# The split activations of a two-layer encoder trunk moved to multiples of 512 bytes in SBUF

## Chip, cores and metric

The kernel runs on one core of one Trainium2 chip. The metric is the device time of one execution in microseconds, over three runs; lower is better.

## The reference, cut to what matters

Two layers work on 256 tokens of 1024 channels in float32. Each layer is a half-weighted SwiGLU feed-forward, a mixer, and a second half-weighted feed-forward; a norm ends the trunk.

```python
def swiglu(x, w_gate, w_up, w_down):
    return (jax.nn.silu(x @ w_gate) * (x @ w_up)) @ w_down      # 1024 -> 2816 -> 1024
...
for l in range(DEPTH):                                           # DEPTH = 2
    x = x + RES_HALF * swiglu(rmsnorm(x, norm_ffn1[l]), ffn1_w_gate[l], ffn1_w_up[l], ffn1_w_down[l])
    h = rmsnorm(x, norm_mix[l])
    gq, gk, gv, gz, gb, ga, c_q, c_kv, k_rope, gate_logits = split_cols(h @ w_in[l])     # 1024 -> 4784
    y_a = gdn_branch(...)     # gated delta rule, both directions, then @ gdn_proj (512 -> 1024)
    y_b = mla_branch(...)     # latent attention (@ mla_w_uq, @ mla_w_ukv), then @ mla_proj (512 -> 1024)
    gates = sigmoid(gate_logits)
    x = x + (gates[:, :, 0] * y_a + gates[:, :, 1] * y_b) @ w_out[l]
    x = x + RES_HALF * swiglu(rmsnorm(x, norm_ffn2[l]), ffn2_w_gate[l], ffn2_w_up[l], ffn2_w_down[l])
return rmsnorm(x, final_norm)
```

## The kernel before, in words

Every large product is made of three float32r passes. An activation a is kept as a high and a low part (`split`, lines 101 to 109), a weight w too (`weights`, lines 111 to 127), and `mm3` (lines 129 to 135) adds a_hi w_hi, a_hi w_lo and a_lo w_hi in PSUM for one chunk of 128 channels and one tile of 128 tokens. In each pass the activation's 128x128 block is the stationary operand, which a weight load (PEld in the profile) brings into TensorE, and the weights' 128 rows of up to 512 columns are the moving operand, which the matmul (PE) streams. TensorE loads the block of the next pass while the columns of this one stream.

The activations lie channel-major: `xh`, `xl` (the normed trunk, 8 chunks of 256 tokens), `hh`, `hl` (the feed-forward's hidden layer, 22 chunks), and the eight `fr2` buffers of the mixer (two chunks each, `fr` in the profile), which hold the latents, the attention's output, the delta rule's output and the merged branches in turn. `to_chan` and `to_chan2` make them with TensorE transposes followed by `split`.

A feed-forward goes through the 2816 hidden columns in blocks of 512: gate, up, transposes into `hh` and `hl`. Then two products with w_down follow, 512 columns each, of 22 chunks x 2 token tiles x 3 passes. The last feed-forward's down products are in `finale`, whose second one takes the weights of its last six chunks from buffers in a pool `fin` of its own (`down(1, second, tail=6, pool=fin)`, line 303). The mixer's products with `xh` are `dense` and `qkv_group`; those with `fr2` are `mla_dense` (latents), and near the mixer's end the calls of `dense_t` on `oT` and `gT` and of `dense_halves` on `yT`. The order of the program's calls in the mixer is written out by hand (lines 980 to 1053); a planner in the framework then places the instructions of each engine by simulated due times.

Weights come through SyncE's DMA queue into `raw` (three buffers), ScalarE writes the high part (line 122), VectorE the low part (line 123).

Pools take SBUF one behind the other: `const`, `main`, `wpool`, `small`; then `ffn` or `mix`, which are opened and closed in turn and begin at the same byte; and `fin` behind `ffn`. Within a pool, tiles lie in the order in which they are first asked for, each rounded up to 32 bytes. The program places these tiles at the following bytes of each partition:

| tile | pool | begins at | past a multiple of 512 |
| --- | --- | --- | --- |
| `ident` | const | 17248 | 352 |
| `x_sb` | main | 23040 | 0 |
| `xh`, `xl` | main | 31232, 39424 | 0 |
| `whi` (3), `wlo` (3) | wpool | from 72192, steps of 4096 | 0 |
| first tile of `small`, which takes 576 bytes | small | 96768 | 0 |
| `hh`, `hl` | ffn | 97344, 119872 | 64 |
| `h` (4) | ffn | from 150592, steps of 2048 | 64 |
| `fr2` (8) | mix | from 181856, steps of 2048 | 96 |
| `whi` (3), `wlo` (3) of the finale | fin | from 171072 and 183360, steps of 4096 | 64 |

One chunk of 128 tokens is 512 bytes, one 128x512 block of weights 2048 bytes, so that each operand of a 512-column pass keeps the remainder of its tile.

Of the kernel before, what the change touches and what calls it, by code (L numbers as in the profile page):

```python
# [11 lines left out]
F32 = mybir.dt.float32  # L12
# [8 lines left out]
P = 128  # L21
D = 1024
S = 256
# [14 lines left out]
def encoder_trunk(ctx: ExitStack, tc: tile.TileContext, x, positions, norm_ffn1, ffn1_w_gate, ffn1_w_up,  # L38
# [23 lines left out]
    # the tensor engine's clock rises while the first loads run  # L62
# [8 lines left out]
    # columns of gains: ffn1 (8 per layer), mix, ffn2, q latent (3), kv latent (2), gdn (1)  # L71
# [21 lines left out]
    xh = main.tile([P, NKC, S], F32R, name="xh")  # L93
    xl = main.tile([P, NKC, S], F32R, name="xl")
# [6 lines left out]
    def split(hi, lo, ps, gain=None):  # L101
        """hi + lo = gain * ps, both exact in float32r."""
        if gain is None:
            A.copy(out=hi, in_=ps)
            V.tensor_tensor(out=lo, in0=ps, in1=hi.bitcast(F32), op=ALU.subtract)
        else:
            A.activation(out=hi, in_=ps, func=AF.Copy, scale=gain)  # L107
            V.scalar_tensor_tensor(out=lo, in0=ps, scalar=gain, in1=hi.bitcast(F32), op0=ALU.mult,  # L108
                                   op1=ALU.subtract)

    def weights(src, nk, w, pool=wpool):
        """A [nk*128, w] slice of weights, as (hi, lo) tiles of up to 1024 elements a partition."""
        raw = wpool.tile([P, 2048], F32, tag="raw", name="raw", bufs=3)
        nc.sync.dma_start(out=raw[:, :nk * w].rearrange("p (k c) -> p k c", c=w),
                          in_=src.rearrange("(k p) c -> p k c", p=P))
        per = 1024 // w
        res = []
        for k0 in range(0, nk, per):
            n = min(per, nk - k0)
            hi = pool.tile([P, 1024], F32R, tag="whi", name="whi", bufs=3)  # L120
            lo = pool.tile([P, 1024], F32R, tag="wlo", name="wlo", bufs=3)
            A.copy(out=hi[:, :n * w], in_=raw[:, k0 * w:(k0 + n) * w])  # L122
            V.tensor_tensor(out=lo[:, :n * w], in0=raw[:, k0 * w:(k0 + n) * w], in1=hi[:, :n * w].bitcast(F32),  # L123
                            op=ALU.subtract)
            for k in range(n):
                res.append((hi[:, k * w:(k + 1) * w], lo[:, k * w:(k + 1) * w]))
        return res

    def mm3(ps, a, w, n, start, stop, ts=range(NT)):
        """ps[t] (+)= a^T w in three passes, for the token tiles ts."""  # L130
        for t in ts:
            a1, a2 = (v[:, t * P:(t + 1) * P] for v in a)
            T.matmul(ps[t][:, :n], lhsT=a1, rhs=w[0], start=start, stop=False)  # L133
            T.matmul(ps[t][:, :n], lhsT=a1, rhs=w[1], start=False, stop=False)  # L134
            T.matmul(ps[t][:, :n], lhsT=a2, rhs=w[0], start=False, stop=stop)  # L135

    def dense_t(acts, src, c0, w, evac, tail=4, pool=wpool):
        """evac(t, psum [128 tokens, w]) of acts @ src[:, c0:c0+w]; acts: (hi, lo) [128, tokens] of each chunk.
        The last chunks (tail or fewer) go through for one token tile, then for the other."""
# [19 lines left out]
    def dense(ah, al, nk, src, c0, w, evac, **kw):  # L159
        dense_t([(ah[:, k, :], al[:, k, :]) for k in range(nk)], src, c0, w, evac, **kw)  # L160

    def dense_halves(acts, parts):
        """dense_t for two parts (src, c0, evac) of 512 columns: the first half of the chunks for both, then the second."""
# [11 lines left out]
    def to_chan(srcs, hi, lo, kc, gain0=None):  # L175
        """Transposes srcs[t] ([128 tokens, n*128]) into chunks kc.. of hi / lo [128, chunk, tokens]."""
        n = srcs[0].shape[1] // P
        for j in range(0, n, 2):
# [6 lines left out]
            if gain0 is None:  # L185
                split(hi[:, kc + j:kc + j + m, :], lo[:, kc + j:kc + j + m, :],
                      pt[:, :m * S].rearrange("p (c s) -> p c s", s=S))
            else:
                for i in range(m):
                    g = gain0 + j + i  # L190
                    split(hi[:, kc + j + i, :], lo[:, kc + j + i, :], pt[:, i * S:(i + 1) * S], gcol[:, g:g + 1])
# [7 lines left out]
    def x_done(t, cg):  # L199
        """Half cg of x's tile t is final: sum of squares."""  # L200
        A.activation(out=junk, in_=x_sb[:, t, cg * 512:(cg + 1) * 512], func=AF.Square,
                     accum_out=state["ss"][:, t, cg:cg + 1])
# [28 lines left out]
    def ffn(w_gate, w_up, w_down, next_gain, hook=None):  # L231
# [3 lines left out]
        with tc.tile_pool(name="ffn", bufs=1) as fp:  # L235
            hh = fp.tile([P, NFC, S], F32R, name="hh")
            hl = fp.tile([P, NFC, S], F32R, name="hl")
            for c0 in range(0, DFF, 512):
# [17 lines left out]
                else:  # L256
                    dense_halves([(xh[:, k, :], xl[:, k, :]) for k in range(NKC)],
# [12 lines left out]
    def finale(down):  # L270
        """The last x, its norm, the result; x of the first half lies by its gains before the second is there."""
# [37 lines left out]
    def mixer_consts(tmp):  # L309
# [16 lines left out]
        alog = const.tile([P, depth, 8], F32, name="alog")  # -exp(A_log)  # L326
# [12 lines left out]
        # m[p, f]  # L339
# [6 lines left out]
        # half[:, 0]: partition % 32 < 16, half[:, 1]: the others  # L346
# [7 lines left out]
        # the off-diagonal 16-blocks of the 32-blocks on the diagonal: below it (mlo) and above it (mup)  # L354
# [11 lines left out]
        # rotary tables  # L366
# [42 lines left out]
    def mixer(l, next_gain):  # L409
# [7 lines left out]
        with tc.tile_pool(name="mix", bufs=1) as mp:  # L417
# [5 lines left out]

            def fr2():
                return mp.tile([P, 2, S], F32R, tag="fr2", name="fr2", bufs=8)
# [8 lines left out]
            def rstd_row():  # L434
                """rstd along the free axis, the same in every partition."""
# [26 lines left out]
            def to_chan2(srcs, gains):  # L462
                """Chunks of 128 channels, two to a tile: a list of (hi, lo) [128, tokens]."""
                n = srcs[0].shape[1] // P
                res = []
                for j in range(0, n, 2):
# [13 lines left out]
                    res += [(hi[:, i, :], lo[:, i, :]) for i in range(m)]  # L480
# [18 lines left out]
            def gdn_scalars():  # L499
# [4 lines left out]
                # softplus(a) = max(a, 0) + log1p(exp(-|a|))  # L504
# [14 lines left out]
            qkT = mp.tile([P, 8, S], F32, name="qkT")  # L519
            vT = {}  # lies in ysb until ysb is written  # L520
# [4 lines left out]
            def qkv_group(grp):  # L525
                """Two of the twelve chunks of channels."""
# [3 lines left out]
                # one group of sums after the other: they share a bank. The second takes the weights from the last on  # L530
                for c in range(2):
                    cc = slice(c * P, (c + 1) * P)
                    terms = [m for kc, (wh, wlo) in enumerate(ws)
                             for m in ((wh, xh[:, kc, :]), (wh, xl[:, kc, :]), (wlo, xh[:, kc, :]))]
                    for i, (w, a) in enumerate(terms[::-1] if c else terms):
                        T.matmul(pc[:, c], lhsT=w[:, cc], rhs=a, start=(i == 0), stop=(i == len(terms) - 1))  # L536
# [16 lines left out]
                # 2 silu(.); the lengths and |k| v below take account of the 2  # L553
# [5 lines left out]
            def lengths(c0):  # L559
                """1/|.| of four of the eight heads of q and k, a column for each head."""  # L560
                pss = gdp()[:, :4 * NT * 32].rearrange("p (c t s) -> p c t s", c=4, t=NT)
                for c in (0, 2):
# [3 lines left out]
                    for g in range(4):  # L566
                        # the sums for the tokens of group g, in each of its partitions
# [28 lines left out]
            def mla_dense(hf):  # L596
                """q, k, v of four heads, token-major, rotary parts turned."""
# [22 lines left out]
            def mla_heads(q, k, v):  # L620
                """attend(pair of heads), of the four that q, k, v hold."""
# [15 lines left out]
                def attend(c):  # L637
# [36 lines left out]
                    oT.append((hi[:, c, :], lo[:, c, :]))  # L674
# [4 lines left out]
            LA, Z, egc, cs = {}, {}, {}, {}  # L679
            LAd = {}  # L680
            for d in range(2):
                LAd[d] = mp.tile([P, NT, NH, 2, P], F32, name=f"LA{d}")  # [.., 0, :] for q, [.., 1, :] for k
# [7 lines left out]
            def gdn_coeffs():  # L690
# [3 lines left out]
                # -beta / |k|^2  # L694
# [17 lines left out]
            def gdn_decay(t):  # L712
                """E[j, h, i]: decay from token j to token i of the tile, 0 where i comes before j."""
                for d in range(2):
# [10 lines left out]
                    if t == d:  # L725
                        # first tile of this direction: decay of each token up to the carried state
# [5 lines left out]
                    # hi_m[p, f] holds where f is at or after p in this direction  # L732
# [25 lines left out]
            def gdn_base():  # L758
                """XC, ZC: inverses (and transposes) of the 16-blocks on the diagonal, each block in a partition of its
                own meanwhile."""  # L760
# [47 lines left out]
            def inv_zero():  # L808
                """Z = X^T = (1 + L)^-T from the inverted 16-blocks: blocks of 32, 64, 128 in turn."""
# [23 lines left out]
            def inv2(d):  # L833
# [9 lines left out]
                # the 64-block that the last step takes X from  # L843
# [41 lines left out]
            def gdn_first(d):  # L885
                """First tile of direction d: its solution, and what it adds to the other tile."""
# [39 lines left out]
            def gdn_out(t):  # L926
# [10 lines left out]
                # o here is -|q| sqrt(128) times the true one, zs_t is 2 silu(z) / rstd  # L937
# [118 lines left out]
    new_norm()  # L1056
    state["squares"] = False  # of the input: once its products run
# [32 lines left out]
```

## Time and profile before

| | us |
| --- | --- |
| median of the three runs | 1267.02 |
| lowest and highest | 1266.68, 1269.48 |
| span of the profiled execution, first to last instruction | 1260.2 |
| the median less that span | 6.8 |
| TensorE busy in the span | 1230.4 |
| VectorE busy | 774.1 |
| ScalarE busy | 623.4 |
| GpSimd busy | 132.5 |

The runs shown give a time for the median only; the profiled execution is known by its span, and what lies around a span (start and end of the program) is taken as the 6.8 us above. A matmul's recorded duration (390 ns for 512 columns) overlaps the next one's, so the pace of the matmuls is read from their start times. Nothing else runs on the core.

### The profile page before, as it was taken

How to read it: one execution, taken by the hardware profiler on the slowest of the kernel's cores; microseconds unless marked ns; L12 is line 12 of the kernel's file. 1: busy time of each engine (PE TensorE's matmuls, PEld its weight loads, DVE VectorE, ACT ScalarE, POOL GpSimd, SP SyncE). 2: the span in 40 equal slices, each digit the busy share in tenths (PEclk: the TensorE clock that was granted, in tenths of full speed). 3: DMA queues.
4: the chain of work that ended last, by engine and by line, in shares of the span. 5: the costliest groups of instructions: out<-in, count | busy, mean ns of one | idle time of the engine just before them, and what ended most of it. 6: DMA issues, size and time to landing. Idle time of an engine off the chain costs nothing.

```text
span 1260.2 us, 17612 instructions
## 1 busy us (share of the span) xinstructions
PE 1230.4 (98%) x7064; PEld 1031.9 (82%) x7064; DVE 774.1 (61%) x1127; ACT 623.4 (49%) x911; POOL 132.5 (11%) x237
## 2 busy tenths in 40 slices
PE   9999999899999999999999999998999999999997
PEld 6888889777988788888888888897778787888886
DVE  5655556986757665554555554588876576555554
ACT  6554445546445455443445443465555455544443
POOL 1000001445001000000000000015540000000010
PEclk9999999999999999999999999999999999999999
DMA  7554554435222555555555555543442245565552
GB/s 266 175 197 153 198 184 157 153 119 167 71 99 95 164 176 181 187 169 198 182 187 182 185 167 201 177 147 123 150 162 74 68 134 184 168 199 179 188 184 84
DMA packets 114576, 202.70 MB, mean 161 GB/s; under 512 B 4107, under 2 KB 30399, under 8 KB 114495
## 3 DMA queue, kind: packets, MB, share of 16 engines
q1 hardware_dynamic: 114031, 200.52, 47.8%
q8 instruction: 55, 0.90, 0.3%
q10 hardware_dynamic: 464, 1.06, 0.2%
q14 instruction: 26, 0.21, 0.1%
HBM read 200.52 MB, written 1.05 MB: 160 GB/s over the span
## 4 chain that ended last, share of the span: by engine, by line
PE 88%; DVE 4%; POOL 4%; issue 1%; ACT 1%; DMA 0%; POOLq 0%; SPq 0%; ACTq 0%
PE acc L133 24%; PE acc L134 23%; PE acc L135 23%; PE acc L536 4%; PE ms L183 2%; DVE wlo L123 2%; POOL bt L783 1%; PE ms L671 1%; PE ms L642 1%; POOL t L785 1%; PE gd L134 1%; PE gd L135 1%; PE gd L133 1%; PE gd L912 1%; DVE cv L551 1%
## 5 line engine op out<-in xcount | busy, mean ns | idle before, releaser
L123 DVE TENSOR_TENSOR wlo<-raw,whi 128x1024 fp32r<-128x1024 f32 (+3 forms) x388 | 471.2, 1217 | 371.0 <-ACT whi L122 369.0
L122 ACT CAST whi<-raw 128x1024 fp32r<-128x1024 f32 (+3 forms) x388 | 398.8, 1031 | 435.9 <-PE acc L135 392.0
L134 PE MATMUL acc<-wlo,xh 128*128 128x512 f32 (+3 forms) x968 | 360.7, 374 | 0.0
L135 PE MATMUL acc<-whi,xl 128*128 128x512 f32 (+3 forms) x968 | 357.5, 372 | 0.0
L133 PE MATMUL acc<-whi,xh 128*128 128x512 f32 (+3 forms) x968 | 344.9, 376 | 0.1
L134 PEld LDWEIGHTS acc<-wlo,xh 128*128 128x128 f32 x968 | 182.4, 188 | 29.8 <-issue 0.4
L133 PEld LDWEIGHTS acc<-whi,xh 128*128 128x128 f32 x968 | 181.4, 188 | 30.4 <-ACT xh L107 0.8
L135 PEld LDWEIGHTS acc<-whi,xl 128*128 128x128 f32 x968 | 182.1, 188 | 29.3
L134 PE MATMUL acc<-wlo,hh 128*128 128x512 f32 x352 | 138.9, 395 | 0.0
L135 PE MATMUL acc<-whi,hl 128*128 128x512 f32 x352 | 138.7, 394 | 0.0
L133 PE MATMUL acc<-whi,hh 128*128 128x512 f32 x352 | 129.1, 397 | 0.0
L135 PEld LDWEIGHTS acc<-whi,hl 128*128 128x128 f32 x352 | 65.9, 187 | 16.1
L133 PEld LDWEIGHTS acc<-whi,hh 128*128 128x128 f32 x352 | 65.9, 187 | 15.9
L134 PEld LDWEIGHTS acc<-wlo,hh 128*128 128x128 f32 x352 | 65.9, 187 | 15.3
L133 PE MATMUL acc<-whi,fr 128*128 128x512 f32 (+1 forms) x152 | 60.9, 407 | 9.2 <-DVE pre L543 7.9
L134 PE MATMUL acc<-wlo,fr 128*128 128x512 f32 (+1 forms) x152 | 61.0, 404 | 0.0
L135 PE MATMUL acc<-whi,fr 128*128 128x512 f32 (+1 forms) x152 | 58.2, 400 | 2.3 <-DVE fr L108 2.3
L536 PE MATMUL acc<-xl,whi 128*128 128x256 f32 x192 | 55.6, 289 | 0.0
L536 PE MATMUL acc<-xh,whi 128*128 128x256 f32 x192 | 55.5, 291 | 0.0
L536 PE MATMUL acc<-xh,wlo 128*128 128x256 f32 x192 | 53.3, 288 | 0.0
L551 DVE SCALAR_TENSOR_TENSOR cv<-pre,ccol,cv 128x256 f32<-128x256 f32 x96 | 51.6, 569 | 0.0
L246 ACT ACTIVATE sil<-acc,rstd 128x512 f32<-128x512 f32 (+1 forms) x48 | 31.0, 654 | 29.5 <-PE acc L135 29.4
(298 smaller groups left out, 1273.3 us busy)
## 6 DMA issues: line engine op xcount, KB each, us to landing
raw<-in_ffn_w_up_dram SPq DMA_DIRECT2D x40, 1024.0 KB, 4.9
raw<-in_ffn_w_down_dram SPq DMA_DIRECT2D x40, 1024.0 KB, 4.9
raw<-in_ffn_w_gate_dram SPq DMA_DIRECT2D x38, 1024.0 KB, 4.9
raw<-in_w_in_dram SPq DMA_DIRECT2D x32, 1024.0 KB, 4.8
raw<-in_w_out_dram SPq DMA_DIRECT2D x8, 1024.0 KB, 4.8
raw<-in_ffn_w_gate_dram SPq DMA_DIRECT2D x12, 512.0 KB, 3.5
raw<-in_ffn_w_up_dram SPq DMA_DIRECT2D x8, 512.0 KB, 3.5
raw<-in_ffn_w_down_dram SPq DMA_DIRECT2D x8, 512.0 KB, 3.3
```

What stands on the lines that cost most here:

```text
L122: A.copy(out=hi[:, :n * w], in_=raw[:, k0 * w:(k0 + n) * w])
L123: V.tensor_tensor(out=lo[:, :n * w], in0=raw[:, k0 * w:(k0 + n) * w], in1=hi[:, :n * w].bitcast(F32), op=ALU.subtract)
L133: T.matmul(ps[t][:, :n], lhsT=a1, rhs=w[0], start=start, stop=False)
L134: T.matmul(ps[t][:, :n], lhsT=a1, rhs=w[1], start=False, stop=False)
L135: T.matmul(ps[t][:, :n], lhsT=a2, rhs=w[0], start=False, stop=stop)
L183: T.transpose(out=pt[:, i * S + t * P:i * S + (t + 1) * P], in_=srcs[t][:, (j + i) * P:(j + i + 1) * P], identity=ident)
L246: A.activation(out=sil[t][:, :w], in_=ps, func=AF.Silu, scale=rstds[0][:, t:t + 1])
L536: T.matmul(pc[:, c], lhsT=w[:, cc], rhs=a, start=(i == 0), stop=(i == len(terms) - 1))
L551: V.scalar_tensor_tensor(out=cv[:, c], in0=pre[:, c, d:d + S], scalar=wc, in1=cv[:, c], op0=ALU.mult, op1=ALU.add)
L642: T.matmul(sc[:, t * S:(t + 1) * S], lhsT=qT[:, t * P:(t + 1) * P], rhs=kT, start=True, stop=True)
L671: T.matmul(po[r:r + MV, :S], lhsT=v[:, kk, h, :], rhs=prT[:, kk, :], start=(kk == 0), stop=(kk == NT - 1))
L783: G.tensor_tensor(out=tv, in0=M[:, b + 1:16, b:b + 1].to_broadcast([P, na, nb]), in1=Y[:, b:b + 1, 0:nb].to_broadcast([P, na, nb]), op=ALU ...
```

## The change

A tile of 448 bytes that nothing reads, `align`, is put first into `small`, and GpSimd clears it once. Two of the eight `fr2` buffers are asked for at the top of the mixer, so that all eight lie first in `mix`; the first two calls of `fr2()` hand them out. `xh`, `xl`, `hh`, `hl` get a shape with the token tile as an axis of its own ([128, chunks, 2, 128] for [128, chunks, 256], the same bytes), and what reads or writes them is written in that shape. Comments and docstrings go.

```diff
+    align = small.tile([P, 112], F32, name="align", bufs=1)
+    G.memset(align, 0.0)
...
-    xh = main.tile([P, NKC, S], F32R, name="xh")
-    xl = main.tile([P, NKC, S], F32R, name="xl")
+    def pitched(pool, n, name):
+        return pool.tile([P, n, NT, P], F32R, name=name)
+
+    xh = pitched(main, NKC, "xh")
+    xl = pitched(main, NKC, "xl")
...
     def mm3(ps, a, w, n, start, stop, ts=range(NT)):
...
-            a1, a2 = (v[:, t * P:(t + 1) * P] for v in a)
+            a1, a2 = (v[:, t, :] for v in a)
...
     def to_chan(srcs, hi, lo, kc, gain0=None):
...
-                split(hi[:, kc + j:kc + j + m, :], lo[:, kc + j:kc + j + m, :],
-                      pt[:, :m * S].rearrange("p (c s) -> p c s", s=S))
+                split(hi[:, kc + j:kc + j + m], lo[:, kc + j:kc + j + m],
+                      pt[:, :m * S].rearrange("p (c t s) -> p c t s", t=NT, s=P))
...
-                    split(hi[:, kc + j + i, :], lo[:, kc + j + i, :], pt[:, i * S:(i + 1) * S], gcol[:, g:g + 1])
+                    split(hi[:, kc + j + i], lo[:, kc + j + i],
+                          pt[:, i * S:(i + 1) * S].rearrange("p (t s) -> p t s", s=P), gcol[:, g:g + 1])
...
-            hh = fp.tile([P, NFC, S], F32R, name="hh")
-            hl = fp.tile([P, NFC, S], F32R, name="hl")
+            hh = pitched(fp, NFC, "hh")
+            hl = pitched(fp, NFC, "hl")
...
+            def fr2_tile():
+                return mp.tile([P, 2, S], F32R, tag="fr2", name="fr2", bufs=8)
+
+            frs = [fr2_tile(), fr2_tile()]
+
             def fr2():
-                return mp.tile([P, 2, S], F32R, tag="fr2", name="fr2", bufs=8)
+                return frs.pop() if frs else fr2_tile()
...
             def qkv_group(grp):
...
-                             for m in ((wh, xh[:, kc, :]), (wh, xl[:, kc, :]), (wlo, xh[:, kc, :]))]
+                             for m in ((wh, xh[:, kc]), (wh, xl[:, kc]), (wlo, xh[:, kc]))]
...
-                        T.matmul(pc[:, c], lhsT=w[:, cc], rhs=a, start=(i == 0), stop=(i == len(terms) - 1))
+                        T.matmul(pc[:, c].rearrange("p (t s) -> p t s", s=P), lhsT=w[:, cc], rhs=a, start=(i == 0),
+                                 stop=(i == len(terms) - 1))
```

## Rows read from the trace of the kernel before

**Rows 1.** The page: busy time by engine; the granted clock in 40 slices

```profile
PE 1230.4 (98%) x7064; PEld 1031.9 (82%) x7064; DVE 774.1 (61%) x1127; ACT 623.4 (49%) x911; POOL 132.5 (11%) x237
...
PEclk9999999999999999999999999999999999999999
```

**Rows 2.** The page: the chain that ended last, by engine

```profile
PE 88%; DVE 4%; POOL 4%; issue 1%; ACT 1%; DMA 0%; POOLq 0%; SPq 0%; ACTq 0%
```

**Rows 3.** Windows, all engines: stretches of products with xh, hh, xh, fr, hh, hh

```profile
85.28:102.96 17.68, 17.68 (x79) 14.59 (x78) 10.08 (x10) 7.64 (x9) 0.00 (x0) 1.00 0.63 204
141.86:164.26 22.40, 22.40 (x97) 17.95 (x96) 10.63 (x10) 8.38 (x9) 0.00 (x0) 1.00 0.56 197
395.83:400.36 4.53, 4.53 (x21) 3.75 (x20) 2.84 (x14) 3.84 (x14) 2.02 (x2) 1.00 0.31 119
400.36:402.94 2.58, 2.58 (x12) 2.07 (x11) 2.58 (x6) 1.62 (x2) 0.00 (x0) 1.00 0.00 0
1216.10:1244.33 28.23, 28.23 (x122) 22.63 (x121) 15.37 (x14) 12.48 (x15) 3.53 (x2) 1.00 0.44 162
1245.49:1252.98 7.49, 7.49 (x34) 6.20 (x33) 1.94 (x4) 1.43 (x3) 1.85 (x2) 1.00 0.00 0
```

**Rows 4.** Timeline, TensorE: xh after transposes (start, duration, what)

```profile
80.69 0.40 PE L134 MATMUL acc<-wlo,xh 128*128 128x512 f32 x1
...
82.55 0.40 PE L133 MATMUL acc<-whi,xh 128*128 128x512 f32 x1
82.78 0.82 PE L183 MATMUL ms<-ident,h 128*128 128x128 f32 x6
...
83.67 0.39 PE L135 MATMUL acc<-whi,xl 128*128 128x512 f32 x1
...
85.06 0.39 PE L135 MATMUL acc<-whi,xl 128*128 128x512 f32 x1
```

**Rows 5.** Groups by line and form: products with hh and fr

```profile
L134 PE MATMUL acc<-wlo,hh 128*128 128x512 f32 x352 | 138.9, 395 | 0.0
L134 PE MATMUL acc<-wlo,fr 128*128 128x512 f32 x128 | 50.9, 400 | 0.0
L134 PE MATMUL gd<-wlo,fr 128*128 128x512 f32 x16 | 6.5, 407 | 0.0
L133 PE MATMUL acc<-whi,fr 128*128 128x384 f32 x24 | 10.1, 419 | 7.9 <-DVE pre L543 7.9
```

**Rows 6.** The chain that ended last, in order of time, around mla_dense

```profile
256.42 1.73 POOL cv L564
258.14 1.98 POOL pr L721
261.10 2.23 POOL g L733
266.12 0.66 POOL m L593
267.38 2.96 POOL rqk L576 x2
```

**Rows 7.** Timeline: GpSimd and TensorE at the start

```profile
0.80 0.20 POOL masks.py:197 MEMSET ident<- 128x128 f32 x1 [0.29 <-POOLq L1076]
1.29 0.29 POOL masks.py:199 TENSOR_SCALAR_AFFINE_SELECT ident<-ident 128x128 f32<-128x128 f32 x1
5.21 0.28 PE L85 MATMUL ms<-ident,grow 16*128 16x16 f32 x1
```

**Rows 8.** Tile fr on ScalarE; timelines: last and first uses of shared bytes

```profile
L107 ACT ACTIVATE fr<-ms,gcol x14: 455/474/691, 222.6 to 1026.2; 128x256 fp32r<-128x256 f32 x10, 128x512 fp32r<-128x512 f32 x4
198.04 0.40 PE L135 MATMUL acc<-whi,hl 128*128 128x512 f32 x1
443.88 0.39 PE L135 MATMUL gd<-whi,fr 128*128 128x512 f32 x1
472.75 1.08 ACT L104 CAST hh<-ms 128x512 fp32r<-128x512 f32 x2 [1.77 <-PE ms L183]
```

**Rows 9.** Timeline, TensorE: six transposes of x_sb

```profile
442.99 0.82 PE L183 MATMUL ms<-ident,x_sb 128*128 128x128 f32 x6
```

**Rows 10.** Groups by line and form: moving operands of one run and of two

```profile
L642 PE MATMUL ms<-qk 96*128 96x256 f32 x64 | 17.3, 392 | 0.0
L741 PE MATMUL gd<-qkT 128*128 128x256 f32 x32 | 8.4, 385 | 0.4 <-DVE qkT L556 0.4
```

**Rows 11.** Windows, TensorE alone: the two mixers

```profile
200.00:440.00 240.00, 229.85 (x1692) 0.98 0.38 125
822.00:1062.00 240.00, 229.73 (x1709) 0.99 0.39 128
```

More of the change, by code (lines that the diff above doesn't have):

```diff
@@ L159, in dense @@
     def dense(ah, al, nk, src, c0, w, evac, **kw):
-        dense_t([(ah[:, k, :], al[:, k, :]) for k in range(nk)], src, c0, w, evac, **kw)
+        dense_t([(ah[:, k], al[:, k]) for k in range(nk)], src, c0, w, evac, **kw)
     def dense_halves(acts, parts):
@@ L256, in ffn @@
                 else:
-                    dense_halves([(xh[:, k, :], xl[:, k, :]) for k in range(NKC)],
+                    dense_halves([(xh[:, k], xl[:, k]) for k in range(NKC)],
                                  [(w_gate, 0, ev_gate), (w_up, 0, ev_up)])
@@ L479, in to_chan2 @@
                             split(hi[:, i, :], lo[:, i, :], pt[:, i * S:(i + 1) * S], gains[j + i])
-                    res += [(hi[:, i, :], lo[:, i, :]) for i in range(m)]
+                    res += [tuple(v[:, i, :].rearrange("p (t s) -> p t s", s=P) for v in (hi, lo)) for i in range(m)]
                 return res
@@ L673, in attend @@
                     split(hi[:, c, :], lo[:, c, :], po[:, :S])
-                    oT.append((hi[:, c, :], lo[:, c, :]))
+                    oT.append(tuple(v[:, c, :].rearrange("p (t s) -> p t s", s=P) for v in (hi, lo)))
                 return attend
```

## The prediction

> **What bounds the kernel now.** I read the page first. TensorE is busy for 1230.4 of 1260.2 us, at full clock throughout, and the next engine for 774.1 [rows 1]; the chain that ended last is TensorE for 88% [rows 2]. A matmul's busy time overlaps its neighbour's, so these shares do not tell whether the matmuls could follow each other faster. For that I read start times, in stretches in which TensorE did nothing but 512-column passes, and divided the distance from the first start to the last by the number of steps (the count of a window less one, since a window also counts the matmul that runs when it opens). The reader is to see two paces in the rows [rows 3]:
>
> - Gate and up, stationary operand `xh`/`xl`: 17.68 us over 78 steps, 226.7 ns.
> - Down, stationary operand `hh`/`hl`: 22.40 us over 96 steps, 233.3 ns.
>
> The columns are the same 512, the weights come from the same buffers. The makers of weights are no slower in the second stretch: VectorE is busy for 10.63 of 22.40 us there and for 10.08 of 17.68 us in the first, ScalarE for 8.38 and 7.64, the DMA share is 0.56 against 0.63. So the slower stretch is the less loaded one, and the step of 6.6 ns belongs to the pass itself.
>
> What differs is the place. By the table of places, `xh` and the weights both begin at a multiple of 512 bytes, `hh` 64 bytes past one, `fr2` 96 bytes past one. Two more pairs of rows separate the place from all else:
>
> - In one place of the mixer TensorE goes without a gap from `xh` to `fr2`: 4.53 us over 20 steps (226.5 ns), then 2.58 us over 11 steps (234.5 ns) [rows 3].
> - In the last down product the stationary operand stays `hh`, but the last six chunks (36 passes) take their weights from the pool `fin`, where they begin 64 bytes past a multiple, as `hh` does. The pace before is 28.23 us over 121 steps, 233.3 ns, and in these chunks 7.49 us over 33 steps, 227.0 ns [rows 3]. The other engines are quieter there, but that is not what makes passes fast: under the mixer's `xh` passes, at 226.5 ns, ScalarE is busy for 3.84 of 4.53 us.
>
> So a pass is fast where the block being loaded and the columns being streamed stand alike within 512 bytes, and slow where they do not, in steps of about 16 cycles of 2.4 GHz. It is the difference of the two places that counts, since with both at 64 it is fast.
>
> One thing speaks for less. After transposes the aligned `xh` passes run slowly too for a while: from 80.69 to 82.55 us 8 steps of 232.5 ns, from 83.67 to 85.06 us 6 steps of 231.7 ns, and only then 226.7 [rows 4]. An aligned stream can thus be slow for some 18 passes before it settles. An unaligned one does not settle within the 96 steps above.
>
> **The change, part by part.**
>
> *Place of hh and hl.* `small` takes 576 bytes now and 1024 afterwards, so `ffn` begins at 97792, which is 191 x 512, and `hl`, 22528 (44 x 512) further on, also at a multiple. Their 512-column passes number 3 x 352 = 1056 [rows 5]; the 36 with weights from `fin` are fast already and stay so, because `fin` moves by the same 448 bytes and its weights then begin at 171520 = 335 x 512, like `hh`. That leaves 1020. Fully settled, each gives back 6.6 ns. In gate and up a block of 96 passes has some 18 slow ones, which makes its mean (78 x 226.7 + 18 x 231.7) / 96 = 227.6 and the gain 5.7; a down product has 132 passes and transposes only around its ends. I take 6.0 ns: 1020 x 6.0 = 6.1 us. Bounds 5.8 and 6.7 us. These stretches are TensorE without idle time, so all of it shows in the end. The weights can follow: gate and up ask for as many weights per pass at 226.7 ns and get them [rows 3].
>
> *Place of fr2.* As the first tiles of `mix` the eight buffers begin at 97792 and steps of 2048. Their 512-column passes number 3 x (128 + 16) = 432 [rows 5]. The 48 in `mla_dense`, and the 72 of 384 columns, lie where GpSimd and VectorE lead the chain [rows 6]; I count them at nothing. The other 384 run at the mixer's end, back to back but with transposes in between. There I take 5.0 ns of the 7.9 that the mixer's rows show: 1.9 us. Bounds: 0, if the mixer's other chains swallow it, and 384 x 7.9 = 3.0 us.
>
> *The other tiles of mix and ffn.* All of them move by 448 bytes within 512, so pairs of operands inside one pool stand to each other as before. Only partners in `const` (`ident` above all) stand differently. Transposes show no such dependence: six of `h`, at 64, take 0.82 us, and six of `x_sb`, at 0, also 0.82 us [rows 4, 9]. Nothing counted. VectorE's and ScalarE's writes of the parts are not on the path in these stretches, by the busy times above.
>
> *The shape with the token tile apart.* The bytes are contiguous, so a merged pattern is what it was. If it stayed in two runs of 128, the nearest row is the plain float32 product whose moving operand is two such runs: 385 ns for 256 columns against 392 ns for one run [rows 10]. Nothing.
>
> *The cleared filler.* One GpSimd instruction at the start, of about the size of the clearing of `ident`, 0.20 us. It can be in front of `ident`, which is finished at 1.58 us and first used at 5.21 us [rows 7]: 3.6 us of cover, under the wait for the first loads. Without that cover it would cost 0.2 us.
>
> *Waits on shared bytes.* `fr2` now lies where `hh` lay, so its first write in a mixer must follow the last pass on `hl`: that starts at 198.04 us, the first write at 222.6 us. In the second feed-forward the first write of `hh` must follow the last pass on `fr2`: 443.88 against 472.75 us [rows 8]. Both have over 20 us to spare; behind either write would stand ScalarE's weight parts. Nothing.
>
> *Sum.* 6.1 + 1.9 = 8.0 us off the profiled span of 1260.2 us, to about 1252.2 us. What lies around the span in the median's time, 6.8 us, stays, so 1267.0 - 8.0 = 1259.0 us. By the bounds the gain is 5.8 to 9.7 us, 1257.3 to 1261.2 us.
>
> The Trainium skill speaks against all this: "SBUF — State Buffer", section "Who interferes with whom", gives TensorE two independent read ports, one for the moving operand and one for weight loads, and says that TensorE never waits on anyone. By that the places of the two operands could not matter, and the change would leave 1267 us. The change of pace inside the last down product disagrees with it.
>
> **The rivals.**
>
> *The place is not the cause.* Then something else makes `hh` and `fr2` slower, and the time is 1267.0 us. For it: `xh` passes can be slow too. Against it: the last down product, where only the weights' buffers change. 5%. This is also what the skill's rule gives.
>
> *The aligned stream does not settle.* The passes on `hh` stay at the 231.7 to 232.5 ns of the stretch after transposes. Gain 1404 x 1.3 = 1.8 us, so 1265.2 us. For it: that stretch. Against it: the 78 steps that follow, and `finale`. 5%.
>
> *The planner orders the mixer differently.* New places and a new instruction can shift its simulated dues. The place is the mixer between 200 and 440 us and its twin, where TensorE stands idle for 10.2 and 10.3 us now [rows 11], behind GpSimd and VectorE [rows 6]. If a worse order doubles that idle time, it costs 20.4 us, and the result is 1259.0 + 20.4 = 1279.4 us, slower. It decides from 4.0 us per mixer on, when the gain is gone. Against it: no dependence that orders these chains is changed. 5%.
>
> **How the numbers follow.** The forecast has 85%. A difference under 0.2% (2.5 us) can hardly be told from none here. The forecast's own range is its bounds with 1.3 us on either side, about half of what the three runs lie apart: 1256.0 to 1262.5 us. The 8-in-10 range keeps the lower end and goes on to 1264.0 us, for a stream that settles late. Faster by over 0.2%: the 85% and half of the stream that settles late, 0.87; within 0.2%: 0.08; slower: 0.05.
>
> **What would show it.** Down stretches at 227 ns a pass, and the last six chunks no longer different from the chunks before them; the mixer's end at 227 to 230 ns; `xh` stretches unchanged; the order of the passes the same; about 6 us less in the four down stages together, 2 us less in the two mixers. It would be wrong if down stays at 233 ns, or if the mixers' idle time grows.

## The result, and the profile after

The changed kernel takes 1257.95 us (median of 9 runs, 1257.24 to 1259.63), the kernel before, run beside it, 1266.68 us (9 runs, 1260.14 to 1269.48). The ratio is 0.9945, with a 95% interval from 0.9923 to 0.9966: 7.0 us less, between 4.3 and 9.8 us. The medians alone lie 8.7 us apart.

The page of the kernel after: span and instructions, busy time by engine, the granted clock in 40 slices, and the chain that ended last by engine. They answer to [rows 1, 2].

```profile
span 1255.5 us, 17613 instructions
...
PE 1225.0 (98%) x7064; PEld 1036.0 (83%) x7064; DVE 774.5 (62%) x1127; ACT 624.1 (50%) x911; POOL 132.7 (11%) x238
...
PEclk9999999999899999999999999998999999999999
...
PE 88%; DVE 4%; POOL 4%; issue 1%; ACT 1%; DMA 0%; POOLq 0%; SPq 0%; ACTq 0%
```

Nothing has changed place: TensorE is busy for 98% of the span, holds 88% of the chain, and issues the same 7064 matmuls, in the same order of tiles. The span and TensorE's busy time, 5.4 us less, say that less time passed, and two slices of the clock row that were 9 are 8.

Windows of the kernel after, TensorE alone, over the stretches of [rows 3] in the same order (products with `xh`, `hh`, `xh`, `fr`, `hh`, `hh`). Columns: stretch and its length, busy time (instructions that it touches), granted clock, share of the DMA engines, GB/s.

```profile
85.09:102.78 17.69, 17.69 (x79) 1.00 0.65 203
141.56:163.33 21.77, 21.77 (x97) 1.00 0.58 196
395.43:400.00 4.57, 4.57 (x21) 1.00 0.29 112
400.00:402.50 2.50, 2.50 (x12) 1.00 0.00 0
1212.30:1239.73 27.43, 27.43 (x122) 1.00 0.47 170
1240.86:1248.34 7.48, 7.48 (x34) 1.00 0.00 0
```

Each window goes from the start of one pass to the start of a later one, so its length divided by the steps is the pace, and one touched instruction more than steps belongs to it. The first line is 78 steps of `xh`: 226.8 ns, as before. The second, 96 steps of `hh`, fell from 22.40 to 21.77 us, 233.3 to 226.7 ns. The third, 20 steps of `xh` in the mixer, has 228.5 ns where it had 226.5: its first nine steps, right behind other work, go at 224 to 236 ns and the others at 226 to 227. The fourth, 11 steps of `fr`, fell from 234.5 to 227 ns. In the last two, the 121 steps of down fell from 233.3 to 226.7 ns a pass, and the 33 steps whose weights lie in `fin`, at 227.0 ns before, are now like all the others.

The first stage as a whole, on TensorE's timeline of the kernel after: the first pass on `hh`, and the first pass behind the down product.

```profile
135.14 0.40 PE L141 MATMUL acc<-whi,hh 128*128 128x512 f32 x1
...
196.47 0.28 PE L550 MATMUL acc<-xh,whi 128*128 128x256 f32 x1
```

In the trace of before these two start at 135.35 and 198.28 us. The down product took 62.93 us and takes 61.33 us: 1.60 us less. The four down stages, worked out in the same way, gave back 1.59, 1.59, 1.59 and 1.45 us, together 6.2 us. A group's busy time shows this poorly: for the 352 passes of `wlo,hh` it went from 138.9 to 137.4 us, 395 to 390 ns for one.

```profile
L142 PE MATMUL acc<-wlo,hh 128*128 128x512 f32 x352 | 137.4, 390 | 0.0
```

Those 390 ns contain the overlap with the neighbours, and their end is modelled. Only the distance from start to start is the cost.

The span fell by 4.7 us only, from 1260.2 to 1255.5 us. The rest was lost again in the mixers. Spans and mean granted clocks of three profiled executions, as the view of the cores lists them: the kernel before as it stands ahead of the prediction, the kernel before profiled again (`before_again`, below), and the kernel after.

```profile
core 0: 1260.2 us, clock 0.993
```
```profile
core 0: 1265.2 us, clock 0.988
```
```profile
core 0: 1255.5 us, clock 0.990
```

One kernel gives spans 5.0 us apart, and the longer one has the lower clock. The clock falls at places in the mixers. Windows of TensorE around three of them, first before, then after:

```profile
324.00:338.00 14.00, 14.00 (x319) 0.88 0.01 2
866.00:878.00 12.00, 6.91 (x28) 0.86 0.25 93
944.00:950.00 6.00, 6.00 (x149) 1.00 0.29 112
```
```profile
324.00:338.00 14.00, 14.00 (x247) 0.76 0.01 2
866.00:878.00 12.00, 9.24 (x39) 0.72 0.19 49
944.00:950.00 6.00, 6.00 (x105) 0.72 0.01 3
```

The column behind the count is a mean of the two levels, 2.4 and 1.2 GHz: 0.76 over 14 us is 2 x 0.24 x 14 = 6.7 us at the lower one, 0.88 is 3.4 us. In the profiled execution of after, the three places have 3.4 us more at half clock each, 10.2 us together. By the start times of the same matmuls in both traces, the extra stretches took back 1.5, 1.2 and 1.5 us, so that the later products on `fr2`, 1.0 us shorter in each mixer, can't be seen in the mixers' own lengths. What TensorE did before the clock fell differs. In the kernel after, before the falls at 867.7 and at 325.0 us:

```profile
860.70:867.70 7.00, 2.93 (x12) 1.00 0.32 123
318.00:325.00 7.00, 7.00 (x151) 1.00 0.42 150
```

Before the first it had mostly been idle. Before the second the profile shows no idle time: it was at the attention's products, at 256-column passes and at the delta rule's products of 32x32 blocks.

The same comparison without the chance of one profile: each run lists its time with the mean granted clock of that execution. Over the 74 executions of the kernel before that ran beside the experiments below (1259.4 to 1270.0 us, clocks 0.984 to 0.995), a straight line gives 1.02 us for each 0.001 of clock. For the 21 of the kernel after it gives 0.89 us. At one and the same clock the lines are 8.2 us apart at 0.988, 7.9 us at 0.990 and 7.4 us at 0.994. The medians of all these executions, 1263.81 and 1258.23 us, are only 5.6 us apart. The mean clock of the changed kernel's executions is lower, 0.9890 against 0.9909, which by these lines gives back 1.6 to 1.9 us. Clocks of 0.993 or more came in 33 of 74 executions before, and in 3 of 21 after.

### The profile page after: what moved, and what is told of

Its sections match the earlier page's. It is cut to its first block, busy times and chain, and to the rows that moved or that the text cites. A ratio compares the mean times of both kernels' runs of the same rounds, so it can differ in the third digit from the quotient of the medians.

```text
span 1255.5 us, 17613 instructions
## 1 busy us (share of the span) xinstructions
PE 1225.0 (98%) x7064; PEld 1036.0 (83%) x7064; DVE 774.5 (62%) x1127; ACT 624.1 (50%) x911; POOL 132.7 (11%) x238
## 4 chain that ended last, share of the span: by engine, by line
PE 88%; DVE 4%; POOL 4%; issue 1%; ACT 1%; DMA 0%; POOLq 0%; SPq 0%; ACTq 0%
PE acc L141 24%; PE acc L142 23%; PE acc L143 23%; PE acc L550 4%; PE ms L191 2%; DVE wlo L131 2%; POOL bt L798 1%; PE ms L686 1%; PE ms L657 1%; POOL t L800 1%; PE gd L141 1%; PE gd L142 1%; PE gd L143 1%; PE gd L927 1%; DVE cv L566 1%
## 5 line engine op out<-in xcount | busy, mean ns | idle before, releaser
L142 PE MATMUL acc<-wlo,hh 128*128 128x512 f32 x352 | 137.4, 390 | 0.0
```

## The experiments

Theory: what counts is how the stationary block and the moving columns stand to each other. Rivals: the place of each by itself counts; something that came with the change but is not the place; a slow start that the aligned stream keeps; a new order in the mixer. Nine more kernels were run, one of them in two runs (`off_256`), and both kernels of the comparison once more. Each time below that is called *at equal clock* is the mean of the kernel's executions against the line through the 74 executions of before, at that kernel's mean clock. Those 74 scatter around their line by 0.6 us (standard deviation), and a clock listed to 0.001 leaves 0.5 us open in a single run.

| run | places within 512 bytes: `xh` / `hh` / `fr2` / weights | median us (runs) | ratio, 95% interval | at equal clock |
|---|---|---|---|---|
| before_again | 0 / 64 / 96 / 0 | 1266.88 (1) | | |
| ffn_only | 0 / 0 / 32 / 0 | 1261.22 (10) | 0.9976, 0.9955 to 0.9996 | -6.4 |
| fr_only | 0 / 64 / 0 / 0 | 1261.41 (10) | 0.9985, 0.9968 to 1.0002 | -2.1 |
| all_64 | 64 / 64 / 64 / 64 | 1257.71 (10) | 0.9946, 0.9925 to 0.9966 | -8.4 |
| off_32 | 0 / 32 / 32 / 0 | 1266.75 (1) | | +0.2 |
| off_128 | 0 / 128 / 128 / 0 | 1265.44 (1) | | -1.1 |
| off_256 | 0 / 256 / 256 / 0 | 1253.38 (1) | | -8.1 |
| off_256_timed | 0 / 256 / 256 / 0 | 1258.31 (12) | 0.995, 0.993 to 0.9969 | -8.1 |
| xh_64 | 64 / 64 / 96 / 0 | 1272.25 (6) | 1.0089, 1.0053 to 1.0125 | +9.2 |
| after_again | 0 / 0 / 0 / 0 | 1258.4 (12) | 0.9948, 0.9929 to 0.9967 | -8.1, both sets of runs |
| w256_64 | as after; 64 for weights of 256-column products | 1254.07 (6) | 0.9923, 0.9892 to 0.9953 | -9.8 |
| w256_0 | as after; 256 for the same weights | 1257.93 (12) | 0.9955, 0.9934 to 0.9977 | -8.4 |

Ratios are against the kernel before, run beside each on the same chip.

**before_again: how fixed is a pace?** The kernel before, with nothing changed.

> The kernel before, unchanged, to see what varies between its executions, whose times lie between 1260 and 1269 us. If the pace of the unaligned passes is fixed by the places, the down stretches run at 233 ns a pass again and a time over 1262 us comes from elsewhere, for example from more stretches at half the clock (the profiled execution before had four: two of 6.8 us and two of 3.4 us). If the pace is set anew in each execution, a longer execution shows down passes at more than 233 ns, and xh stays at 227.

Windows of TensorE, 96 steps of `hh` and 11 of `fr`:

```profile
142.00:164.40 22.40, 22.40 (x97) 1.00 0.56 197
401.68:404.25 2.58, 2.58 (x12) 1.00 0.00 0
```

The lengths are those of [rows 3], although the span is 5.0 us longer. The paces were not set anew in this execution; what differs is time at half clock, 0.988 against 0.993 in the mean. The run's time, 1266.88 us, is 1.7 us over its span, and in every listed execution of either kernel that distance is 1.7 to 1.8 us.

**ffn_only and fr_only: each part alone.** The first puts only the filler into `small`. The mixer's pool moves with it, and its `fr2` buffers then stand at 32. The second moves only `fr2`.

```diff
 ffn_only, against before:
+    align = small.tile([P, 112], F32, name="align", bufs=1)
+    G.memset(align, 0.0)
 fr_only, against before:
+            fill = mp.tile([P, 112], F32, name="fill")
+            G.memset(fill, 0.0)
+
+            def fr2_tile():
+                return mp.tile([P, 2, S], F32R, tag="fr2", name="fr2", bufs=8)
+
+            frs = [fr2_tile(), fr2_tile()]
+
             def fr2():
-                return mp.tile([P, 2, S], F32R, tag="fr2", name="fr2", bufs=8)
+                return frs.pop() if frs else fr2_tile()
```

> Only the filler in small: hh and hl at a multiple of 512, fr2 at 32 past one. Place theory: down passes at 227 ns, each of the four down stages shorter by 1.5 to 1.6 us (6.2 us together), fr2 passes still at about 234 ns, the time about 6 us under the kernel before. If the place is not the cause: down stays at 233 ns and the time is that of the kernel before.

> The filler is first in mix instead, followed by the eight fr2 buffers: fr2 at a multiple of 512, hh and hl stay at 64 past. Place theory: fr2 passes at about 228 ns, the mixers together about 2 us shorter apart from changes in the clock, down at 233 ns, the time about 2 us under the kernel before. If the place is not the cause: fr2 passes stay at 234 ns.

Windows of TensorE of `ffn_only` (96 steps of `hh`, 11 of `fr`, 121 of the last down product), then of `fr_only` (96 steps of `hh`, 11 of `fr`):

```profile
142.87:164.63 21.76, 21.76 (x97) 1.00 0.56 201
401.32:403.88 2.56, 2.56 (x12) 1.00 0.00 0
1216.50:1244.54 28.04, 27.75 (x122) 1.00 0.47 165
```
```profile
141.75:164.15 22.40, 22.40 (x97) 1.00 0.60 199
403.61:406.10 2.49, 2.49 (x12) 1.00 0.00 0
```

Each part speeds up its own products (226.7 and 226.6 ns) and leaves the other's slow (232.8 ns for `fr` at 32, 233.3 ns for `hh` at 64). At equal clock they give 6.4 and 2.1 us, 8.5 together, where the change gives 8.1. The ratios as measured show less: the executions of `ffn_only` had a mean clock of 0.987, and the interval of `fr_only` reaches past 1, so that its part rests on the paces and on the comparison at equal clock.

The third line of `ffn_only` has 0.29 us without a pass and is 0.61 us longer than after's. That is a wait, told below with `off_256`, where it is the same.

**all_64: the place, or the difference?** The changed kernel with 64 bytes in front of everything, so that all the operands begin at 64, and none at a multiple of 512.

```diff
+    off = main.tile([P, 16], F32, name="off")
+    G.memset(off, 0.0)
     junk = main.tile([P, 512], mybir.dt.bfloat16, name="junk")
```

> The changed kernel with 64 bytes more in front of main, so that xh, the weights, hh and fr2 all stand 64 past a multiple of 512. If it is the difference of the two operands' places within 512 bytes that counts: 227 ns everywhere, the time of the changed kernel, about 1258 us. If each operand itself has to begin at a multiple of 512 bytes: all 512-column passes at about 233 ns, 3900 passes x 6 ns = 23 us more than the changed kernel, about 1281 us.

Windows of TensorE: 78 steps of `xh`, 96 of `hh`, 11 of `fr`.

```profile
85.24:102.93 17.69, 17.69 (x79) 1.00 0.63 204
141.70:163.46 21.76, 21.76 (x97) 1.00 0.56 199
402.20:404.70 2.49, 2.49 (x12) 1.00 0.00 0
```

All are as fast as with everything at 0. "Aligned to 512" is not the cause: the difference of the two operands is. The rival of the place by itself is out.

**off_32, off_128, off_256: which differences?** The changed kernel with a filler of another length (120, 16 or 48 floats in place of 112), so that `hh` and `fr2` stand 32, 128 or 256 bytes away from the weights.

```diff
-    align = small.tile([P, 112], F32, name="align", bufs=1)
+    align = small.tile([P, 48], F32, name="align", bufs=1)
```

> The changed kernel with a filler of 480 bytes, so that hh, hl and fr2 stand 32 past a multiple of 512 while the weights stand at 0. If any difference within 512 bytes is slow: down at 233 ns, fr2 at 233 to 234 ns (the fr2 passes of the run with the filler in small alone stood at 32 and took 233.1). If only differences of 64 and more count for hh: 227 ns.

> The same with a filler of 64 bytes: hh, hl and fr2 at 128 past, the weights at 0. If the period is 512 bytes: 233 ns. If a period of 128 bytes counts: 227 ns for hh.

> The same with a filler of 192 bytes: hh, hl and fr2 at 256 past, the weights at 0. If the period is 512 bytes: 233 ns. If it is 256 bytes or a divisor of it: 227 ns. A half period might also be the place where the two streams are farthest apart, and then be faster than 227 ns.

Windows of TensorE, in each kernel 96 steps of `hh`; for the last also 121 steps of the last down product.

```profile
141.84:164.24 22.40, 22.40 (x97) 1.00 0.56 197
```
```profile
142.67:165.07 22.40, 22.40 (x97) 1.00 0.61 197
```
```profile
141.76:163.53 21.76, 21.76 (x97) 1.00 0.57 200
...
1207.86:1235.87 28.00, 27.73 (x122) 1.00 0.47 165
```

32 and 128 bytes are as slow as 64, 256 is as fast as 0. So 256 bytes is enough of a period, not 512, and a filler of 192 bytes would do. Between 32 and 128 bytes there is no gradual change: 233.3 ns in all three. A half period that is faster still, which the last expectation held possible, does not show. Differences between 128 and 256 bytes were not run.

The last line has a surprise: 28.00 us for what takes 27.43 us in the kernel after. Its steps are 0.22 and 0.23 us nearly throughout, and one place takes the difference. The waits of `off_256` from 1225 to 1236 us (engine, line and what it waited for: total, times, longest):

```profile
ACT whi L130 <- DMA raw<-in_ffn_w_down_dram: 3.6, 1, 3.6
DVE wlo L131 <- ACT whi L130: 3.4, 1, 3.4
PEld acc L142 <- DVE wlo L131: 0.7, 1, 0.7
```

The last load of weights for `down` but one is issued at 1220.83 us and lands at 1227.21 us, 6.4 us later. ScalarE waits for it for 3.6 us, then splits five pieces in a row, VectorE behind it, and the weight load of TensorE waits 0.7 us for the fifth. In the kernel after the load lands 5.7 us after its issue, and the chain of the same engines, in the window from 1229 to 1240 us, ends ahead of TensorE:

```profile
DVE wlo L131 <- ACT whi L130: 4.2, 2, 2.7
ACT whi L130 <- DMA raw<-in_ffn_w_down_dram: 2.9, 1, 2.9
```

No wait of TensorE stands there, but little is left: the piece is ready 0.35 us ahead of its pass in this trace and 0.23 us in that of `after_again`, against 0.68 and 1.08 us in the two of the kernel before. All other kernels with fast passes on `hh` have the wait at the same pass: `ffn_only`, `all_64`, both runs of `off_256`, `w256_64` and `w256_0`, six of eight profiles, 0.3 to 0.6 us each by the start times. None of the six profiles with slow passes has it. The new pace has used up the weights' reserve at this place.

**off_256_timed and after_again: is 256 worth as much as 0?** The kernel of `off_256` and the changed kernel, timed beside each other in five rounds.

> hh, hl and fr2 at 256 past a multiple of 512 once more, timed. If the period is 256 bytes: the time of the changed kernel within 2 us, passes at 227 to 228 ns. If 512 bytes are needed: about 8 us slower than the changed kernel.

> The changed kernel once more. If the passes gain 8 us and the rest of the difference between executions is time at half the clock, its passes go at 227 to 228 ns again, and its span less 0.4 us for each us at half the clock is 1244 us, as in its first profile (1255.5 less 0.4 x 28.1), against 1252 us of both profiles of the kernel before. Timed beside it: 6 to 8 us faster than the kernel before. If the change itself brings more time at half the clock, its profile shows 28 us of it or more again.

1258.31 and 1258.40 us, 12 runs each, are the same time. The short run of `off_256` was one with a clock of 0.993. Beside the kernel before (1264.23 us), `after_again` is 5.8 us faster by the medians and 6.6 us by the ratio. Its profile repeats that of the kernel after: a span of 1255.4 us, and the clock down at the same places for the same times, which was the sign named for a change that itself brings more time at half clock. The two profiles of `off_256`, with the same paces, have spans of 1251.7 us and clocks of 0.993 and 0.994: the pace does not bring it in every execution.

**xh_64: the sign reversed.** The kernel before, with `xh` and `xl` put 64 bytes on as well and the weights left where they were. The products with `xh` then stand like those with `hh`.

```diff
+    off = main.tile([P, 16], F32, name="off")
+    G.memset(off, 0.0)
+    offw = wpool.tile([P, 112], F32, name="offw", bufs=1)
+    G.memset(offw, 0.0)
     xh = main.tile([P, NKC, S], F32R, name="xh")
```

> The kernel before with xh and xl moved to 64 past a multiple of 512, while the weights stay at 0 and hh, fr2 at 64 and 96: no pair stands alike except in the last six chunks. Place theory: the xh passes of 512 columns, some 2400, go from 227.6 to about 233.1 ns, 13 us more, about 1279 us against 1265 of the kernel before. If hh and fr2 are slow for a reason of their own: xh stays at 227 ns and the time is that of the kernel before.

Windows of TensorE: 78 steps of `xh`, and 67 steps of the 256-column products with `xh`; then those 67 steps in the kernel before. (A recorded 256-column matmul, some 290 ns long, reaches over two later starts, so that these windows touch more instructions than start in them.)

```profile
86.99:105.20 18.20, 18.20 (x79) 1.00 0.63 204
...
129.67:137.37 7.70, 7.70 (x71) 1.00 0.81 267
```
```profile
127.11:135.23 8.12, 8.12 (x70) 1.00 0.71 261
```

The products with `xh`, at 226.7 ns until now, went to 233.4 ns at will. The sign and the place were right, the size was not: 9.2 us more at equal clock where 13 were expected, and the second line shows most of the reason. The 256-column passes became faster, 121.2 to 114.9 ns. In one gate and up stage the 512-column passes lost 2.7 us and the 256-column ones won 0.6 us; over the whole trace the means go from 227.6 to 233.3 ns (2314 steps) and from 119.7 to 115.9 ns (910 steps), 9.7 us in sum. That was in no theory.

**w256_64 and w256_0: are 256 columns better apart?** The changed kernel, with the weights of all products of 256 columns put 64 or 256 bytes into their buffer. The diff is that of `w256_64`; `w256_0` has 64 in place of 16 in the slices. For room, two small tiles of the mixer, `rows` and `tb`, share a buffer in both.

```diff
-            hi = pool.tile([P, 1024], F32R, tag="whi", name="whi", bufs=3)
-            lo = pool.tile([P, 1024], F32R, tag="wlo", name="wlo", bufs=3)
+            hi = pool.tile([P, 1152], F32R, tag="whi", name="whi", bufs=3)
+            lo = pool.tile([P, 1152], F32R, tag="wlo", name="wlo", bufs=3)
+            if w == 256:
+                hi, lo = hi[:, 16:], lo[:, 16:]
...
-                rows = t2("rows", 1, (P, 2, 4 * NT * 32))
+                rows = t2("th", 1, (P, 2, 4 * NT * 32))
...
-                            tb = t2("tb", 1, (P, N8, 32))
+                            tb = t2("th", 1, (P, N8, 32))
```

> The changed kernel with room for 128 more columns in each weight buffer; products of 256 columns put their weights 64 bytes past a multiple of 512, all others stay at 0. With all xh at 64 the 256-column passes of a gate-and-up stage had gone from 122 to 116 ns. If unlike places are faster for 256 columns: 116 ns for the 384 passes of the feed-forwards' last blocks and the 576 of the short convolution's products, up to 3.5 us less than the twin whose weights stand at 256, at an equal share of the clock. If they are not: 120 to 122 ns and no difference.

> The same buffers and the same order, but the weights of 256-column products stand at 256 past a multiple of 512, which counts as alike. 256-column passes at 120 to 122 ns, 512-column passes at 227, the time that of the changed kernel within 2 us.

Windows of TensorE over the same 67 steps, in `w256_64` and in `w256_0`:

```profile
127.76:135.74 7.98, 7.98 (x71) 1.00 0.75 264
```
```profile
126.90:135.01 8.11, 8.11 (x71) 1.00 0.77 266
```

119.1 against 121.0 ns here. Over the whole traces the 256-column steps have a mean of 117.0 and 119.6 ns, and with some 900 such steps that is 2.3 us. At equal clock the twins are 1.4 us apart (-9.8 and -8.4), where up to 3.5 us were expected. With 6 and 12 runs the two intervals overlap, so the size is not settled, but the paces are apart in the trace. Of the kernels timed in several runs `w256_64` has the lowest median, 1254.07 us, 7.8 us below the kernel before that ran beside it (1261.88 us). Of the 3.9 us between the medians of the twins a part is the higher mean clock of its six runs, 0.9905 against 0.9883.

## Why the prediction was right, and where it was not

**The mechanism.** The pace of a 512-column pass depends on how its stationary block and its moving columns stand to each other. Shown: it follows `hh` alone (`ffn_only`), `fr2` alone (`fr_only`), can be switched off for `xh` (`xh_64`), and doesn't follow the places themselves (`all_64`). The Trainium skill, "SBUF — State Buffer", section "Who interferes with whom", gives TensorE two independent read ports and lets it wait on nobody. The measured paces disagree with that as far as this kernel goes, since two reads that never meet would leave no room for a difference: 226.7 and 233.3 ns for the same instructions, with only the difference of two addresses changed.

**Place of hh and hl.** 6.1 us was forecast; the four down stages gave back 6.2 us, and `ffn_only` 6.4 us at equal clock. Over the whole trace the steps between passes on `hh` went from 233.1 to 227.1 ns in the mean, the 6.0 ns that were taken. That the weights can follow was too simple, since gate and up show it only for their own place: the weights keep up in both profiles of the changed kernel, with 0.2 to 0.35 us left at one pass of the last stage, and come too late there in the six others with this pace.

**Place of fr2.** 1.9 us was forecast; by the start times the late products gave 1.0 us in each mixer, and `fr_only` gave 2.1 us at equal clock. The 5.0 ns taken for a pass were a little low: over the whole trace the mean step went from 234.0 to 228.0 ns. The 48 and 72 passes that were counted at nothing add nothing that could be told apart.

**Shape, filler, shared bytes.** Counted at nothing, and nothing shows. The clearing of `align` takes 0.19 us at the start, ahead of `ident`'s [rows 7], and the first pass on `hh` still starts at 135.14 us against 135.35. The 256-column passes of `qkv_group`, whose patterns were rewritten, have a mean step of 119.9 to 120.0 ns in the first mixer in two profiles of before, and of 120.0 ns in two of after (steps under 200 ns).

**Within 512 bytes.** This was too coarse. 256 apart is as good as 0. The number of the forecast doesn't hang on it, the filler's length does.

**The step that failed: "What lies around the span in the median's time, 6.8 us, stays."** It is 1.7 to 1.8 us in every execution. The other 5.1 us were no cost around the span: the profiled execution was a short one, and the three times shown were all of longer ones. Behind this lies a misreading: "at full clock throughout" was read from a row of tenths [rows 1], while that execution has a mean clock of 0.993, some 18 us at half clock, and [rows 11] show 0.98 and 0.99 in the mixers. The forecast of the span, about 1252.2 us, so missed by 3.3 us, since after's profiled execution had more time at half clock (0.990 against 0.993). The forecast of the median, 1259.0 us, came within 1.1 us, because the gain was right (8.0 us; 7.4 to 8.2 us at equal clock) and because the median that it was taken from is that of an execution of clock 0.988 by the line above, like most of after's. The second half of this is luck. With a before of 1263.81 us, the median of the 74 executions, the same sum would have given 1255.8 us, 2.4 us below after's 1258.23 us. The part that was not forecast is the lower mean clock of the new kernel's executions.

**The rivals.** That the place is not the cause is out by `ffn_only`, `fr_only` and `xh_64`. That the aligned stream doesn't settle is out: it runs at 226.7 ns over 96 and over 121 steps. The longer last stage of `ffn_only` and `off_256`, which looks like it in a window's mean (28.00 / 121 = 231.4 ns), is one wait for weights. A new order in the mixer is out: the tiles come in the same order. The mixers' idle time, the sign that was named for it, stayed, as the windows of the kernel after over the stretches of [rows 11] show:

```profile
200.00:440.00 240.00, 229.72 (x1685) 0.97 0.39 125
822.00:1062.00 240.00, 229.85 (x1694) 0.98 0.39 125
```

10.3 and 10.2 us idle, as before, but at 0.97 and 0.98 of the clock where before had 0.98 and 0.99.

**Open.** What in the reads makes a pair with unlike places slower, and why 256 columns want the opposite, no run here tells. Nor is it shown why the changed kernel's executions have the lower mean clock more often (3 of 21 at 0.993 or more, against 33 of 74); that is a count, and nothing was run on its cause. It is not this one kernel's chance: of all 56 listed executions of kernels with `xh`, `hh`, `fr2` and the weights alike and nothing else changed in their paces (the kernel after in both runs, `all_64`, `off_256` in both, `w256_0`), 7 reach 0.993, and so do 1 of 20 of `ffn_only` and `fr_only` and 1 of 6 of `xh_64`, which is slower.

## What to carry to other kernels

Where a product loads new weights for each pass, compare the start-to-start distance of its passes with that of another product of the same shape in the same trace. If they differ, compare the operands' byte addresses modulo 256: for 512 columns alike was 6.6 ns a pass faster here, and one filler tile sets it. Before a change of under 1% is read from two profiles or a few runs, put the mean granted clock beside each time and compare at equal clock; here one kernel's own times spread over 10.7 us, more than the change is worth. After a product has been made faster, look at the waits for its weights: a mean over a stretch hides a single late load.

## What was not expected of the hardware

- 512-column passes in these settled stretches have a fast and a slow pace and nothing in between: 226.7 ns with the operands 0 or 256 bytes apart, 233.3 ns on `hh` at 32, 64 and 128 bytes. On `fr2` the slow pace is 232.8 ns at 32 bytes and 234.5 ns at 96.
- For 256 columns it is the reverse, in one stretch of 67 steps: 121.0 to 121.2 ns alike, 119.1 ns with the weights 64 bytes on, 114.9 ns with the activations 64 bytes on. The last two are both 64 bytes apart and still differ.
- Executions of one unchanged kernel lie between 1259.4 and 1270.0 us, with mean granted clocks of 0.995 and 0.984, at 1.02 us for each 0.001.
- The clock fell at 325.0 us in the kernel after although TensorE is shown as busy for 7.00 of the 7.00 us before.
